# The scores' product with the lower part of q in two 64-row halves of the array, and narrower products of zeros at the start

## The chip, the cores and the metric

The kernel runs on one core of a Trainium2 chip. The metric is the device time of one execution in microseconds (us), the median of several runs. One further execution is recorded by the hardware profiler; every start, duration and wait below comes from that one.

## The reference, cut to what matters

The program is one layer of an encoder: 512 rows of 1024 channels, three branches (a convolution, a differential attention, a spatial gate) that are mixed, and an MLP behind them. The change concerns the attention's scores. For each of 8 heads there are two maps j, each with a head dimension of 64:

```
sc = jnp.einsum("bqhjd,bkhjd->bhjqk", qblk, kf) * scale   # scale = 64 ** -0.5
sc = sc - slopes * dist
p  = jax.nn.softmax(sc, axis=-1)
a  = p[:, :, 0] - lam * p[:, :, 1]
o  = jnp.einsum("bhqk,bkhe->bqhe", a, vf)
```

Queries are taken in 4 blocks of 128, so there are 8 x 4 x 2 = 64 score tiles of 128 x 512.

## The kernel before, in words

All operands of products are float32 numbers split in two: an upper part, rounded to the format that TensorE multiplies in one pass (`float32r`), and a lower part, the rest. A product of two split numbers is three products: upper with upper, upper with lower, lower with upper. Every product goes through `pe.matmul`, a helper at L58, and every transpose through L62, so the profile has these two lines for all of TensorE's work and tells products apart by the names of their tiles. TensorE executes in the order in which the code is written (`keep_in_program_order`); the order on VectorE (DVE) and ScalarE (ACT) is set by a scheduler when the program is built, from priorities and its own estimate of durations. Names that begin with `w_` are weights, `hh`/`hl` the upper and lower part of the normalized input, `ps_a` and `ps_b` PSUM banks, of which there are four of each kind.

**Scores.** `proj_qk(h)` makes q and k of head h. For map j the 64 channels of q lie on partitions 0 to 63 (j = 0) or 64 to 127 (j = 1) of the product's bank. ScalarE writes the upper part `qh` there and VectorE the lower part `ql`; a DMA on SyncE's queue then copies each to the other 64 partitions, so that both halves hold the same. `kk` of map j holds the upper part of k on the same 64 partitions and the lower part of k on the other 64. One product with K = 128 rows of `qh` against `kk` is therefore upper with upper plus upper with lower, and a second one, `ql` against `kk`, adds lower with upper (and lower with lower). `scores(q)` does this for both maps: four products of 512 columns, two to a bank. VectorE then adds the slope term and takes the minimum, ScalarE takes the exponential.

`head(h)` yields between its steps (four times `scores`, four times `turn`, and so on); between the steps the projections of the next heads are issued as fill, so that TensorE has other products while VectorE and ScalarE work on the scores.

**Start.** While the input is loaded and normalized, `keep_warm(n)` issues n products of a tile of zeros, 512 columns wide: 26 ahead of the first transposes of the normalized input, 3 and 2 further on. `norm_x(t)` normalizes 128 rows (t = 0 to 3): a square sum on ScalarE, a short chain that ends in `hs` on VectorE (L303), eight transposes on TensorE (L62), and the copies `hh` (ScalarE, L223) and `hl` (VectorE, L224). Weights are split by ScalarE (`w_hi`, L150) and VectorE (`w_lo`, L151). The first three weight units are multiplied with rows 0 to 255 before the transposes of t = 2 and t = 3 are all done: unit, transposes of t = 2, unit, transposes of t = 3, unit.

Lines that the change and the prediction touch: the two score products (L500 and L501 of the code, L58 in the profile), L457 and L458 (the two copies by DMA), L275 to L284 (the zeros), L303 and L151 at the start. One more place is needed to read the prediction: the transposes of `prow` (128 rows) and of `cw`, the convolution's weights, which have only 32 rows, at L341 to L344.

Of the kernel before, what the change touches and what calls it, by code (L numbers as in the profile page):

```python
# [16 lines left out]
P = 128  # L17
S = 512
# [30 lines left out]
def encoder_layer(ctx: ExitStack, tc: tile.TileContext, a: dict, out: bass.AP):  # L49
    nc = tc.nc  # L50
# [13 lines left out]
    def mk(name, bufs=1, **kw):  # L64
        return tc.tile_pool(name=name, bufs=bufs, reuse_waits="tile", **kw)

    def f32(ap):
        return ap.bitcast(F32)
# [101 lines left out]
    def bank(tag):  # L170
        return ps["pool"].tile([P, 512], F32, tag=tag, bufs=ps[tag], name=f"ps_{tag}")
# [42 lines left out]
    def to_T(src, hi, lo, tt):  # L214
        for half in range(2):
            b = bank("b")
            for j in range(4):
                kt = half * 4 + j
                pe.transpose(b[:, j * P:(j + 1) * P], src[:, kt * P:(kt + 1) * P], ident)
            b3 = b.rearrange("p (k t) -> p k t", t=P)  # L220
            c = slice(half * 4, half * 4 + 4)
            tk = slice(tt * P, (tt + 1) * P)
            ev = act.activation(hi[:, c, tk], b3, AF.Copy)  # L223
            vec.tensor_tensor(lo[:, c, tk], b3, f32(hi[:, c, tk]), op=ALU.subtract)  # L224
        return ev.ins
# [43 lines left out]
    with mk("p0") as p0:  # L269
        gpre = p0.tile([P, D], F32, tag="gpre", name="gpre")  # L270
        act.dma_start(gpre, a["norm_mix_pre"].partition_broadcast(P))
        warm = p0.tile([P, 1], F32, tag="warm", name="warm")
        act.activation(warm, eps_t, AF.Sqrt)
        zero = p0.tile([P, S], F32R, tag="zero", name="zero")
        vec.memset(f32(zero[:, :]), 0.0)  # L275

        def keep_warm(n):

            b = bank("b")
            for _ in range(n):  # L280
                pe.matmul(b, zero[:, 0:P], zero, start=True, stop=True)

        keep_warm(26)
        xt = []  # L284
        for t in range(TT):
            xx = p0.tile([P, D], F32, tag="xx", bufs=4, name="xx")
            nc.sync.dma_start(xx, x[t * P:(t + 1) * P, :])
            xt.append(xx)
            if t == W0AT:
                load_to(1)  # L290

        evac = {}

        def norm_x(t):
            sq = p0.tile([P, D], F32, tag="sq", bufs=2, name="sq")
            ss = p0.tile([P, 1], F32, tag="ss", bufs=4, name="ss")
            i = act.activation(sq, xt[t], AF.Square, accum_out=ss)
            if t > 1:
                tc.add_manual_dep(i.ins, evac[t - 2].name, mybir.DependencyInfo(
                    mybir.DependencyClass.NoSync, mybir.DependencyReason.DATA), reason="order")  # L300
            r = rstd_of(p0, ss, 1.0 / D)
            hs = p0.tile([P, D], F32, tag="hs", bufs=2, name="hs")
            vec.scalar_tensor_tensor(hs, xt[t], r, gpre, op0=ALU.mult, op1=ALU.mult)  # L303
            evac[t] = to_T(hs, hh, hl, t)


        hT = (hh, hl)
        norm_x(0)
        keep_warm(3)
        norm_x(1)  # L310
        keep_warm(2)
        first = take(3, 0)
        fb = [bank("a") for _ in first]
        for n, w in enumerate(first):
            if n == 0:

                for i, (sw, m) in enumerate(((0, 0), (1, 0), (0, 1))):
                    for kt in range(KT):
                        pe.matmul(fb[0][:, 0:256], w[sw][:, kt], hT[m][:, kt, 0:256], start=i + kt == 0,
                                  stop=(i, kt) == (2, KT - 1))  # L320
            else:
                run(unit_gen(fb[n][:, 0:256], w, hT, slice(0, 256)))
            if n < 2:
                norm_x(2 + n)
        for n, w in enumerate(first):
            run(unit_gen(fb[n][:, 256:512], w, hT, slice(256, 512)))


        rowsrc = [("conv_b", 8), ("conv_ln_g", 8), ("conv_ln_b", 8), ("b_gate", 24), ("subln_g", 1), ("sgu_b", 8)]
        prow = p0.tile([P, P], F32, tag="prow", name="prow")  # L330
        pool.memset(prow, 0.0)
        off, col = 0, {}
        for n, k in rowsrc:
            pool.dma_start(prow[off:off + k, :], a[n].rearrange("(r c) -> r c", c=P) if len(a[n].shape) == 1 else a[n])
            col[n] = off
            off += k
        cw = p0.tile([32, D], F32, tag="cw", name="cw")
        pool.memset(cw, 0.0)
        pool.dma_start(cw[0:CK, :], a["conv_w"])
        pcol = cq.tile([P, P], F32, tag="pcol", name="pcol")  # L340
        b = bank("b")  # L341
        pe.transpose(b[:, 0:P], prow, ident)
        for c in range(KT):
            pe.transpose(b[:, P + c * 32:P + (c + 1) * 32], cw[:, c * P:(c + 1) * P], ident[0:32, 0:32])  # L344
        vec.tensor_copy(pcol, b[:, 0:P])
        convw = cq.tile([P, KT, 32], F32, tag="convw", name="convw")
        vec.tensor_copy(convw, b[:, P:P + KT * 32].rearrange("p (k j) -> p k j", j=32))

        def pc(n, i=0):
            return pcol[:, col[n] + i:col[n] + i + 1]  # L350

        sub08 = cq.tile([P, 1], F32, tag="sub08", name="sub08")
        vec.tensor_scalar(sub08, pc("subln_g"), 1.0 - LAM_INIT, None, op0=ALU.mult)
# [56 lines left out]
    b = bank("a")  # L410
# [33 lines left out]
    def proj_qk(h, got):  # L444


        wq, wk = take(2)
        bq = bank("a")
        yield from unit_gen(bq, wq, hT)
        qh = ap_.tile([P, 2, S], F32R, tag="qh", bufs=2, name="qh")  # L450
        ql = ap_.tile([P, 2, S], F32R, tag="ql", bufs=2, name="ql")
        for j, (s0, s1) in enumerate(((0, 64), (64, 0))):
            src = bq[s0:s0 + 64, :]
            hi, lo = qh[s0:s0 + 64, j], ql[s0:s0 + 64, j]
            act.activation(hi, src, AF.Copy, scale=-SCALE)
            vec.scalar_tensor_tensor(lo, src, -SCALE, f32(hi), op0=ALU.mult, op1=ALU.subtract)
            nc.sync.dma_start(f32(qh[s1:s1 + 64, j]), f32(qh[s0:s0 + 64, j]))  # L457
            nc.sync.dma_start(f32(ql[s1:s1 + 64, j]), f32(ql[s0:s0 + 64, j]))  # L458
        bk = bank("a")
        yield from unit_gen(bk, wk, hT)  # L460
        kk = ap_.tile([P, 2, S], F32R, tag="kk", bufs=2, name="kk")
        for j, (s0, s1) in enumerate(((0, 64), (64, 0))):
            src = bk[s0:s0 + 64, :]
            act.activation(kk[s0:s0 + 64, j], src, AF.Copy)
            vec.tensor_tensor(kk[s1:s1 + 64, j], src, f32(kk[s0:s0 + 64, j]), op=ALU.subtract)
        got["qk", h] = qh, ql, kk
# [18 lines left out]
    def head(h, got):  # L485

        qh, ql, kk = got["qk", h]
# [7 lines left out]
        def scores(q):  # L495
            tk = slice(q * P, (q + 1) * P)
            ex = []
            for j in range(2):
                b = bank("b")
                pe.matmul(b, qh[:, j, tk], kk[:, j], start=True, stop=False)  # L500
                pe.matmul(b, ql[:, j, tk], kk[:, j], start=False, stop=True)  # L501
                m = ap_.tile([P, 1], F32, tag="m", bufs=6, name="m")
                vec.tensor_tensor_reduce(b, b, nal[:, 384 - q * P:896 - q * P], 1.0, 3.0e38,  # L503
                                         ALU.add, ALU.min, m)
                e = ap_.tile([P, S], F32, tag="e", bufs=4, name="e")
                l = ap_.tile([P, 1], F32, tag="l", bufs=6, name="l")
                act.activation(e, b, AF.Exp, bias=m, scale=-1.0, accum_out=l)  # L507
                r = ap_.tile([P, 1], F32, tag="r", bufs=6, name="r")
                vec.reciprocal(r, l)
                ex.append((e, r))  # L510
            c1 = ap_.tile([P, 1], F32, tag="c1", bufs=4, name="c1")
            vec.tensor_tensor(c1, ex[1][1], nlam, op=ALU.mult)
            at = ap_.tile([P, S], F32, tag="at", bufs=4, name="at")
            act.activation(at, ex[0][0], AF.Copy, scale=ex[0][1])
            vec.scalar_tensor_tensor(at, ex[1][0], c1, at, op0=ALU.mult, op1=ALU.add)
            ats[q] = at
# [13 lines left out]
        b = bank("b")  # L530
# [6 lines left out]
        b = bank("b")  # L537
# [16 lines left out]
    for h in range(H):  # L554
        n = 0
# [62 lines left out]
    for h in range(H):  # L618
        next(fill)
        next(fill)  # L620
        b = bank("a")
# [96 lines left out]
    for g in range(KT):  # L718
        (w,) = take(1)
        gc = slice(g * P, (g + 1) * P)  # L720
        b = bank("b")
# [429 lines left out]
    for q in range(1, FT // 4):  # L1151
# [20 lines left out]
        s1 = snap(ba)  # L1172
# [88 lines left out]
    s1 = e_ = v6 = w7 = None  # L1261
    for n, step in enumerate(seq[:-TAIL]):
# [8 lines left out]
        if step == ("p1", 3):  # L1271
            s1 = [snap(b) for b in bd]
# [65 lines left out]
```

## Time and profile before

| | |
|---|---|
| median of 3 runs | 1060.08 us (1059.95 to 1060.1) |
| the profiled execution | 1059.99 us, of which span 1058.2 us |
| TensorE products busy | 1042.6 us of the span (99%) |
| TensorE weight loads busy | 900.0 us (85%) |
| VectorE busy | 827.0 us (78%) |
| ScalarE busy | 580.5 us (55%) |
| mean granted TensorE clock | 0.998 |

A busy share says how long an engine had work, not how long others waited for it. PE stands for TensorE's products, PEld for its weight loads, which run beside products. The end of a product is modelled, some 0.16 us late, so the distance from the start of one to the start of the next is what a product costs in a row of them. The profiled execution lies 0.09 us below the median and has 1.8 us outside the span.

### The profile page before, as it was taken

The numbers are of one execution on the slowest core, as the hardware profiler recorded it, in microseconds if no ns is written. First come the engines' busy times: TensorE is split into PE (matmuls) and PEld (weight loads), VectorE is DVE, ScalarE is ACT, GpSimd is POOL, SyncE is SP. The second block draws the span as 40 slices with busy tenths as digits, with TensorE's granted clock in tenths as the row PEclk, the third lists the DMA queues.
The fourth block names the chain that finished last, engine by engine and source line by source line (L and its number), as shares of the span: only waits on it lengthen the run. The fifth ranks groups of instructions, "written<-read, shape, count | busy, mean of one in ns | idle before, by whom it ended". The sixth has DMA issues, their size and how long they took to land.

```text
span 1058.2 us, 14724 instructions
## 1 busy us (share of the span) xinstructions
PE 1042.6 (99%) x5688; PEld 900.0 (85%) x5688; DVE 827.0 (78%) x1296; ACT 580.5 (55%) x902; POOL 24.3 (2%) x41
## 2 busy tenths in 40 slices
PE   8999999999999999999999999999999999999997
PEld 7989898888878888888888888888999999888885
DVE  6696887968997697999899546457988889867746
ACT  5456677766673752344322493344677787555531
POOL 3000000000000000000000000000000001100000
PEclk9999999999999999999999999999999999999999
DMA  7342323223232333322333214463343319724532
GB/s 227 84 139 61 100 81 100 80 81 87 73 120 87 92 112 90 99 81 80 100 100 99 80 45 135 132 226 138 112 150 101 122 43 265 150 80 139 178 121 80
DMA packets 138391, 118.15 MB, mean 112 GB/s; under 512 B 4166, under 2 KB 116850, under 8 KB 138321
## 3 DMA queue, kind: packets, MB, share of 16 engines
q1 hardware_dynamic: 133120, 103.82, 32.1%
q0 software_dynamic: 4480, 11.82, 4.8%
q10 hardware_dynamic: 720, 1.57, 0.4%
q8 instruction: 44, 0.72, 0.3%
q14 instruction: 27, 0.21, 0.1%
HBM read 108.81 MB, written 4.19 MB: 107 GB/s over the span
## 4 chain that ended last, share of the span: by engine, by line
PE 91%; DVE 5%; ACT 2%; issue 1%; DMA 1%; DVEq 0%; ACTq 0%
PE ps_a L58 69%; PE ps_b L58 19%; PE ps_b L62 3%; DVE w_lo L951 1%; DMA xx<-in_x_dram 1%; DVE us L1257 0%; DVE w_lo L151 0%; ACT y L751 0%; DVE hs L303 0%; DVE jk L827 0%; PE ps_a L62 0%; DVE hl L224 0%; ACT jk L825 0%; DVE jk L1247 0%; DVE rs_s L206 0%
## 5 line engine op out<-in xcount | busy, mean ns | idle before, releaser
L150 ACT ACTIVATE w_hi<-w_raw 128x1024 fp32r<-128x1024 f32 x116 | 122.9, 1059 | 214.0 <-PE ps_a L58 177.4
L58 PE MATMUL ps_a<-hh,w_hi 128*128 128x512 f32 (+1 forms) x536 | 205.4, 385 | 0.0
L58 PE MATMUL ps_a<-hh,w_lo 128*128 128x512 f32 (+1 forms) x536 | 202.9, 381 | 0.0
L58 PE MATMUL ps_a<-hl,w_hi 128*128 128x512 f32 (+1 forms) x536 | 202.5, 380 | 0.0
L372 DVE SCALAR_TENSOR_TENSOR acc<-apad,convw,acc 128x512 f32<-128x512 f32 x232 | 173.5, 748 | 5.0
L151 DVE TENSOR_TENSOR w_lo<-w_raw,w_hi 128x1024 fp32r<-128x1024 f32 x116 | 141.5, 1220 | 41.5 <-ACT w_hi L150 41.2
L58 PEld LDWEIGHTS ps_a<-hh,w_lo 128*128 128x128 f32 x536 | 100.3, 188 | 19.6
L58 PEld LDWEIGHTS ps_a<-hl,w_hi 128*128 128x128 f32 x536 | 100.4, 188 | 18.3
L58 PEld LDWEIGHTS ps_a<-hh,w_hi 128*128 128x128 f32 x536 | 100.4, 188 | 18.2
L58 PE MATMUL ps_a<-ring,w_hi 128*128 128x256 f32 x336 | 57.9, 276 | 0.0
L58 PEld LDWEIGHTS ps_a<-ring,w_hi 128*128 128x128 f32 x336 | 50.6, 188 | 0.0
L58 PE MATMUL ps_a<-h2h,w_lo 128*128 128x256 f32 x176 | 48.8, 277 | 1.4 <-DVE w_lo L951 1.4
L58 PE MATMUL ps_a<-w_hi,hh 128*128 128x256 f32 (+1 forms) x160 | 49.7, 311 | 0.0
L58 PE MATMUL ps_a<-h2h,w_hi 128*128 128x256 f32 x176 | 49.0, 278 | 0.0
L58 PE MATMUL ps_a<-h2l,w_hi 128*128 128x256 f32 x176 | 48.8, 277 | 0.0
L58 PE MATMUL ps_a<-w_hi,hl 128*128 128x256 f32 (+1 forms) x160 | 48.7, 304 | 0.0
L58 PE MATMUL ps_a<-w_lo,hh 128*128 128x256 f32 (+1 forms) x160 | 48.6, 304 | 0.0
L507 ACT ACTIVATE e<-ps_b,m 128x512 f32<-128x512 f32 x64 | 43.4, 681 | 7.3 <-DVE m L503 7.0
L58 PE MATMUL ps_a<-ring,w_lo 128*128 128x256 f32 x168 | 46.5, 277 | 0.2 <-DVE w_lo L951 0.2
L58 PE MATMUL ps_a<-w_hi,ring 128*128 128x512 f32 x144 | 45.5, 389 | 0.0
L503 DVE CUSTOM_DVE_ANT_0 ps_b<-ps_b,al 128x512 f32<-128x512 f32 x64 | 43.5, 698 | 0.5 <-PE ps_b L58 0.2
L951 DVE TENSOR_TENSOR w_lo<-w_raw,w_hi 128x1024 fp32r<-128x1024 f32 x28 | 33.7, 1220 | 8.3 <-ACT w_hi L947 8.3
(304 smaller groups left out, 2431.6 us busy)
## 6 DMA issues: line engine op xcount, KB each, us to landing
w_raw<-in_w_in_dram SPq DMA_DIRECT2D x80, 512.0 KB, 3.7
w_raw<-in_w_ffn_up_dram SPq DMA_DIRECT2D x32, 512.0 KB, 4.6
w_raw<-in_w_ffn_down_dram SPq DMA_DIRECT2D x28, 512.0 KB, 4.1
w_raw<-in_w_proj_attn_dram SPq DMA_DIRECT2D x8, 512.0 KB, 4.0
w_raw<-in_w_proj_sgu_dram SPq DMA_DIRECT2D x8, 512.0 KB, 4.1
w_raw<-in_w_proj_conv_dram SPq DMA_DIRECT2D x8, 512.0 KB, 4.1
w_raw<-in_w_out_dram SPq DMA_DIRECT2D x8, 512.0 KB, 3.6
t<-in_w_ffn_down_dram SPq DMA_DIRECT2D x8, 512.0 KB, 5.7
```

Of the source, the lines that this page charges most:

```text
L58: return tc.keep_in_program_order(nc.tensor.matmul(*args, **kw))
L62: return tc.keep_in_program_order(nc.tensor.transpose(*args, **kw))
L150: act.activation(hi, raw, AF.Copy)
L151: vec.tensor_tensor(lo, raw, f32(hi[:, :]), op=ALU.subtract)
L372: vec.scalar_tensor_tensor(o, apad[:, c, j:j + S], convw[:, c, j:j + 1], acc, op0=ALU.mult, op1=ALU.add)
L503: vec.tensor_tensor_reduce(b, b, nal[:, 384 - q * P:896 - q * P], 1.0, 3.0e38, ALU.add, ALU.min, m)
L507: act.activation(e, b, AF.Exp, bias=m, scale=-1.0, accum_out=l)
L951: order(vec.tensor_tensor(lo, raw, f32(hi[:, :]), op=ALU.subtract))
```

## The change

Three things change. The lower part of q is no longer copied to the other 64 partitions. Its product takes only the 64 partitions on which q's channels lie, for map 0 the rows 0 to 63 and for map 1 the rows 64 to 127 of the array, against the upper part of k on the same rows (lower with lower falls away); and the four products of a step are reordered, first both with `qh`, then both with `ql`, with both banks taken ahead of them. At the start 26 products of zeros become 24, and eight of 128 columns follow in a bank of their own.

```
-        def keep_warm(n):
+        def keep_warm(n, m=S):
 
             b = bank("b")
             for _ in range(n):
-                pe.matmul(b, zero[:, 0:P], zero, start=True, stop=True)
-
-        keep_warm(26)
+                pe.matmul(b[:, 0:m], zero[:, 0:P], zero[:, 0:m], start=True, stop=True)
+
+        keep_warm(24)
+        keep_warm(8, P)
...
             nc.sync.dma_start(f32(qh[s1:s1 + 64, j]), f32(qh[s0:s0 + 64, j]))
-            nc.sync.dma_start(f32(ql[s1:s1 + 64, j]), f32(ql[s0:s0 + 64, j]))
...
+            bs = [bank("b") for _ in range(2)]
             for j in range(2):
-                b = bank("b")
-                pe.matmul(b, qh[:, j, tk], kk[:, j], start=True, stop=False)
-                pe.matmul(b, ql[:, j, tk], kk[:, j], start=False, stop=True)
+                pe.matmul(bs[j], qh[:, j, tk], kk[:, j], start=True, stop=False)
+            for j, r_ in enumerate((slice(0, 64), slice(64, 128))):
+                pe.matmul(bs[j], ql[r_, j, tk], kk[r_, j], start=False, stop=True)
+            for j in range(2):
+                b = bs[j]
```

On TensorE, at the first step of the first head, the program of before has the products of the two maps one after the other (a number behind a name tells buffers apart; what a row waits for stands in brackets):

```order
L58 MATMUL ps_b_803<-kk_766,qh_731 128x512 [waits DMAHW1_49,DVE_49]
L58 MATMUL ps_b_803<-kk_766,ql_732 128x512 [waits DMAHW3_49]
L58 MATMUL ps_b_813<-kk_766,qh_731 128x512 [waits DMAHW4_49,DVE_49]
L58 MATMUL ps_b_813<-kk_766,ql_732 128x512 [waits DMAHW5_49]
L58 MATMUL ps_a_783<-hh_88,w_hi_695 128x512
```

At the same place the changed program has both products with the upper part first, and the next unit behind the two with the lower part:

```order
L58 MATMUL ps_b_808<-kk_771,qh_738 128x512 [waits DMAHW1_49,DVE_49]
L58 MATMUL ps_b_809<-kk_771,qh_738 128x512 [waits DMAHW3_49,DVE_49]
L58 MATMUL ps_b_808<-kk_771,ql_739 128x512
L58 MATMUL ps_b_809<-kk_771,ql_739 128x512
L58 MATMUL ps_a_788<-hh_88,w_hi_702 128x512
```

The product with map 1 of `kk` has moved ahead of the product of map 0 with `ql`, and the two with `ql` wait for nothing of their own. The same swap is made at all 32 steps; the order of the other products on TensorE is the same in both programs.

On VectorE the scheduler's order changes in many places. At the start, behind the lower parts of the first 256 rows, the program of before has this, up to the second `w_lo` (`hs` of L303 is the normalized block t = 2):

```order
L151 TENSOR_TENSOR w_lo<-w_raw,w_hi 128x1024
L203 RECIPROCAL rs_r<-rs_s 128x1
L199 TENSOR_SCALAR rs_v<-ss 128x1
L206 SCALAR_TENSOR_TENSOR rs_s<-rs_v,rs_r 128x1
L210 TENSOR_SCALAR rs_s<-rs_s 128x1
L211 TENSOR_TENSOR rs_r<-rs_r,rs_s 128x1
L303 SCALAR_TENSOR_TENSOR hs<-xx,rs_r,gpre 128x1024
L151 TENSOR_TENSOR w_lo<-w_raw,w_hi 128x1024
```

The changed program has this at the same place (one line number further; `hs` of t = 2 and of t = 3 are its two rows of L304):

```order
L151 TENSOR_TENSOR w_lo<-w_raw,w_hi 128x1024 x2
L203 RECIPROCAL rs_r<-rs_s 128x1
L199 TENSOR_SCALAR rs_v<-ss 128x1
L206 SCALAR_TENSOR_TENSOR rs_s<-rs_v,rs_r 128x1
L203 RECIPROCAL rs_r<-rs_s 128x1
L210 TENSOR_SCALAR rs_s<-rs_s 128x1
L206 SCALAR_TENSOR_TENSOR rs_s<-rs_v,rs_r 128x1
L211 TENSOR_TENSOR rs_r<-rs_r,rs_s 128x1
L210 TENSOR_SCALAR rs_s<-rs_s 128x1
L304 SCALAR_TENSOR_TENSOR hs<-xx,rs_r,gpre 128x1024
L211 TENSOR_TENSOR rs_r<-rs_r,rs_s 128x1
L304 SCALAR_TENSOR_TENSOR hs<-xx,rs_r,gpre 128x1024
```

The second `w_lo` and half of the short chain of t = 3 have moved ahead of `hs` of t = 2, and `hs` of t = 3 follows it at once.

## Rows read from the trace of the kernel before

**Rows 1.** The page: its first line, and its parts 1 and 4

```profile
span 1058.2 us, 14724 instructions
PE 1042.6 (99%) x5688; PEld 900.0 (85%) x5688; DVE 827.0 (78%) x1296; ACT 580.5 (55%) x902; POOL 24.3 (2%) x41
...
PE 91%; DVE 5%; ACT 2%; issue 1%; DMA 1%; DVEq 0%; ACTq 0%
```

**Rows 2.** Waits of PE, 60 to 310 us; six windows' sum, 60 to 300 us

```profile
PE ps_b L58 <- DVE kk L465: 0.4, 1, 0.4
...
sum 240.00, PE 239.55 PEld 204.60 DVE 198.29 ACT 166.53 POOL 0.00; mean PE 39.93 PEld 34.10 DVE 33.05 ACT 27.76 POOL 0.00
```

**Rows 3.** Tile ql: count, shortest/median/longest ns, first and last start

```profile
L58 PE MATMUL ps_b<-kk,ql x64: 388/389/398, 68.0 to 293.9; 128*128 128x512 f32 x64
...
L458 SPq DMA_DIRECT2D ql<-ql x16: 461/462/468, 63.0 to 265.6; - x16
```

**Rows 4.** PE's timeline at one step: start, duration, line, names, rows*columns of the array

```profile
75.11 0.39 PE L58 MATMUL ps_b<-kk,qh 128*128 128x512 f32 x1
...
76.02 0.39 PE L58 MATMUL ps_a<-hh,w_hi 128*128 128x512 f32 x1
```

**Rows 5.** The same timeline at the first step of the first head

```profile
68.03 0.39 PE L58 MATMUL ps_b<-kk,ql 128*128 128x512 f32 x1
68.86 0.50 PE L58 MATMUL ps_b<-kk,qh 128*128 128x512 f32 x1 [0.45 <-DVE kk L465]
69.20 0.40 PE L58 MATMUL ps_b<-kk,ql 128*128 128x512 f32 x1
```

**Rows 6.** Timelines of PE, PEld at cw's 32-row transposes; tile cw as in rows 3

```profile
35.60 0.27 PE L62 MATMUL ps_b<-ident,prow 128*128 128x128 f32 x1
35.80 0.68 PE L62 MATMUL ps_b<-ident,cw 32*128 32x32 f32 x8
36.41 0.50 PE L58 MATMUL ps_a<-hh,w_hi 128*128 128x512 f32 x1
36.74 0.40 PE L58 MATMUL ps_a<-hl,w_hi 128*128 128x512 f32 x1
...
35.50 0.14 PEld L62 LDWEIGHTS ps_b<-ident,prow 128*128 128x128 f32 x1
35.80 0.57 PEld L62 LDWEIGHTS ps_b<-ident,cw 32*128 32x128 f32 x8 [0.16 <-issue]
36.41 0.19 PEld L58 LDWEIGHTS ps_a<-hh,w_hi 128*128 128x128 f32 x1
...
L62 PE MATMUL ps_b<-ident,cw x8: 220/222/244, 35.8 to 36.3; 32*128 32x32 f32 x8
```

**Rows 7.** PE's timeline at four 128-row transposes among products of 256 columns

```profile
204.84 0.60 PE L62 MATMUL ps_b<-ident,at 128*128 128x128 f32 x4
205.19 0.36 PE L58 MATMUL ps_a<-w_hi,hh 128*128 128x256 f32 x1
205.39 0.28 PE L58 MATMUL ps_a<-w_lo,hh 128*128 128x256 f32 x1
```

**Rows 8.** The start: timelines of PE, then DVE

```profile
1.46 8.04 PE L58 MATMUL ps_b<-zero 128*128 128x512 f32 x26 [1.46 <-DVE zero L275]
9.84 1.06 PE L62 MATMUL ps_b<-ident,hs 128*128 128x128 f32 x8 [0.35 <-DVE rs_r L203]
18.69 1.06 PE L62 MATMUL ps_b<-ident,hs 128*128 128x128 f32 x8 [1.52 <-DVE hs L303]
23.16 1.09 PE L62 MATMUL ps_b<-ident,hs 128*128 128x128 f32 x8 [0.54 <-DVE hs L303]
...
16.43 0.15 DVE L203 RECIPROCAL rs_r<-rs_s 128x1 f32<-128x1 f32 x1
17.25 1.28 DVE L303 SCALAR_TENSOR_TENSOR hs<-xx,rs_r,gpre 128x1024 f32<-128x1024 f32 x1
18.45 1.22 DVE L151 TENSOR_TENSOR w_lo<-w_raw,w_hi 128x1024 fp32r<-128x1024 f32 x1
```

## The prediction

> **What bounds the kernel now.** I read the page first, then the waits, then the timelines. The page says that TensorE's products are busy for 99% of the span and that 91% of the chain that ended last is PE [rows 1]; a busy share alone would not prove a bound, since product ends are modelled. The waits do: from 60 to 310 us, where all heads lie, PE waited once, for 0.4 us, and VectorE was busy for 198.29 us of the 240 us from 60 to 300 [rows 2]. So in this stage time is what TensorE needs for its list of instructions: an instruction taken out or made dearer there moves the end by its own price. The start is different: there PE waits for the normalized blocks, 0.35, 1.52 and 0.54 us before three of the four groups of transposes [rows 8], and the order on VectorE sets the time.
>
> **What a score product costs.** Four of them and nothing else stand between 75.11 and 76.02 us [rows 4]: 0.91 / 4 = 0.226 us each (0.39 us is the modelled duration). The 64 products with `ql` [rows 3] make 32 pairs of 0.45 us.
>
> **The pair on two halves.** No row shows two products on different rows of the array, so the second half's price is bounded by nothing and by a whole product, 0.226 us. I take nothing: each half has its own rows, weights and bank, and what a product costs elsewhere in the trace is the time to pass its columns through its rows, which two separate halves can do side by side. That saves 0.226 us a pair, 32 x 0.226 = 7.2 us.
>
> **Going into the halves and out again.** The trace has one place where the array changes from 128 rows to fewer and back: the transposes of `cw`, 32 rows each [rows 6]. From the start of `prow` (35.60) to the start of the second product behind them (36.74) it is 1.14 us. Without any cost of the change it would be: one 128-row transpose, 0.11 us ((0.60 - 0.27) / 3 of the four of [rows 7], the 0.27 from [rows 6]); eight of 32 rows at (0.68 - 0.222) / 7 = 0.065, 0.52 us; one product of 512 columns, 0.226. Together 0.86. So 0.28 us go to the change of rows: 0.09 on the way in (0.20 between 35.60 and 35.80 in place of 0.11) and 0.19 on the way out (0.94 - 0.52 - 0.226). The weight loads show why. `prow`'s load began 0.10 us ahead of its product; the first load of `cw` began with its own product, after 0.16 us without a wait that the profile shows, and so did the first load behind `cw` [rows 6]. A change of rows stops the load ahead. That it isn't the change from transposes back to products is seen in [rows 7]: four 128-row transposes and a product of 256 columns take 205.39 - 204.84 = 0.55 us, 4 x 0.11 plus 0.11, nothing more.
>
> What does an uncovered load cost here? After the wait at 68.86 us the next product starts 0.34 us later in place of 0.226 [rows 5]: 0.11 us. The 0.19 on the way out holds it already. On the way in the narrow transposes of `cw` may have hidden it; a product with `ql` has a longer load, so the entry may be 0.09 + 0.11 = 0.20. The round trip thus lies between 0.28 and 0.39 us, and since `cw`'s products are transposes with shorter loads and the way in for `ql` is between the two, I take the middle, 0.335.
>
> A pair: 0.335 - 0.226 = 0.11 us dearer than before, 32 times 3.5 us (bounds 0.054 and 0.164 a pair, 1.7 to 5.2 us). The change has to win 0.226 with one round trip at each of 32 places; that is the step on which the forecast rests.
>
> **The first step.** In the first head `ql` of map 0 ran from 68.03 us while PE had to wait for `kk` of map 1 until 68.86 anyway [rows 5]. In the changed order the product with `kk` of map 1 stands ahead of it, so it comes out of the wait's cover: +0.2 us, once.
>
> **The copies.** Sixteen DMAs of `ql` leave SyncE's queue, 0.46 us of issue each [rows 3]. Weights queued behind them can be loaded earlier, but PE waits for no load in this stage [rows 2]: 0. The later end of bank 0's product delays VectorE's first minimum of a step by about a product; what hides it is the fill between steps, and if that cover failed it would show as PE waiting for `ps_b` or for `at`.
>
> **The start.** Two edits meet here. (a) 26 products of zeros took 8.04 us and ended at 9.50 [rows 8]; two of 0.226 go and eight narrow ones come. Nothing in the trace is a 128-column product of this kind; it costs no less than a 32-column transpose (0.065) and, I assume, no more than a 512-column product (0.226). That ends the zeros 0.07 to 1.36 us later, of which 0.35 us of idle time absorb the first part. I take the 0.11 of a 128-column transpose: 0.42 later, 0.1 us of it visible, which ScalarE's and VectorE's queues swallow: 0. (b) VectorE's new order puts a second `w_lo` ahead of `hs` of t = 2. That `w_lo` took 1.22 us, and three more short operations come with it; five of them took 0.82 us between 16.43 and 17.25 [rows 8], and since the added ones run in the gaps of a dependent chain I count 0.1 each. `hs` of t = 2 starts 1.5 us later than 17.25, and its transposes at about 20.2 in place of 18.69. The unit behind them kept PE until 23.16 - 0.54 = 22.62; now until 24.1. `hs` of t = 3 then follows at once (two times 1.28 from 18.8, done by 21.4) and is ready, so the 0.54 of waiting vanishes: the transposes of t = 3 start at 24.1 in place of 23.16. Cost 1.0 us; 0.6 if the short operations are free, 2.0 if the narrow zeros cost 0.226 each.
>
> **The sum.** 3.5 + 0.2 + 1.0 = 4.7 us on the profiled execution's 1059.99, which is 0.09 below the median: **1064.7 us** (from 1062.5 with 1.7 + 0.2 + 0.6 to 1067.4 with 5.2 + 0.2 + 2.0). A measurement of this kernel can tell about 0.2%, 2.1 us, from no change; the forecast is slower by 0.44%.
>
> **Rivals.** (1) Faster: the change of rows costs a product nothing, because the 512 columns of `qh` ahead leave more time to load than a transpose of 0.11 us did. Then -7.2 + 1.2 = -6.0 and 1054.0 us. It turns on the round trip: below 0.226 - 1.2 / 32 = 0.19 us the kernel gains. Against it: the load at 36.41 also stood behind 0.5 us of transposes and was not begun early [rows 6]. The Trainium skill's page "TensorEngine Tiling (Array Packing)", section Theoretical Speedup, gives a contract dimension of 64 up to twice the speed, which taken alone is this rival; its Key Properties say that a change of tiling mode drains TensorE. The trace agrees with the second by the 0.20 and 0.33 us between starts in [rows 6], and shows nothing of the first.
>
> (2) Half: only one side is paid, about 0.19 us a trip. Then the pairs give -1.2, the start and first step +1.2: 1060.0 us, no change that can be measured.
>
> (3) Slower still: the halves load their weights one after the other, 0.11 us a pair more, 3.5 us: 1068.2; or they don't run together at all, 7.2 us more: 1071.9. For it speaks only that every product in the trace starts a whole product behind the one ahead. Against these the same skill stands with its page "TensorE: Matmul & The Clock Gate" (Part 3, Measured speedup vs the span model): some 4 ns for each further tile in a pack; no row here shows it, and by it 0.1 us would be added to my sum.
>
> VectorE as a new bound is none: even with 7.2 us less it would be busy for 198.29 of 232.8 us [rows 2].
>
> **Chances.** Forecast 0.37, loads one after the other 0.09, no running together 0.07: slower 0.53. Half 0.14: same. Free change of rows 0.33: faster. The range from 1053.5 to 1068.5 holds all but the last slower case and the tails of the others; the likeliest case's own range is 1062.5 to 1067.4.
>
> **What the changed profile would show.** The forecast is right if the two `ql` products (64 rows) start within a few ns of each other, if the load of the first starts with it and not ahead, and if from the first `qh` of a step to the product behind the pair it takes about 1.0 us in place of 0.91. Rival 1 shows some 0.68 us there, with loads begun during `qh`; no running together shows 1.2 or more. At the start the transposes of t = 2 should begin near 20.2 and those of t = 3 near 24.1, without a wait before the latter. I am wrong if PE's waits in 60 to 310 us grow beyond 1 us, since then the new order on VectorE and ScalarE, not the products, would set the time.

## The result, and the profile after

The changed kernel, called after from here on, takes 1069.99 us (median of four runs, 1067.5 to 1072.65); the kernel before, beside it on the same chip, 1060.01 us (four runs, 1059.88 to 1060.1). The ratio is 1.0082 (95% interval 1.006 to 1.0104): slower by 0.8%, 9.98 us, where 4.7 had been forecast. The time lies above the range. The four runs are 1067.5, 1068.75, 1071.24 and 1072.65 us, and this scatter turned out to be a part of the answer. The profiled execution is the last of them.

The page of the changed kernel, its first line and parts 1 and 4 (they answer to [rows 1]):

```profile
span 1070.9 us, 14675 instructions
...
PE 1055.0 (99%) x5694; PEld 898.1 (84%) x5694; DVE 825.9 (77%) x1296; ACT 582.5 (54%) x902; POOL 24.3 (2%) x41
...
PE 92%; DVE 4%; ACT 2%; DMA 1%; issue 1%; SPq 0%; DVEq 0%; ACTq 0%
```

PE still has the whole chain. Its products are busy for 12.4 us more, although 32 pairs now run side by side. The waits of PE from 60 to 310 us ([rows 2]):

```profile
PE ps_b L58 <- DVE kk L465: 0.7, 1, 0.7
```

One wait, as before, 0.2 us longer (0.68 in place of 0.45, both in the first step). So the new order on VectorE and ScalarE makes PE wait no more in the heads, and what was lost there lies inside PE's own list. The tile `ql` of the changed kernel (columns as in [rows 3]), and the idle time ahead of its instructions:

```profile
L58 PEld LDWEIGHTS ps_b<-kk,ql x64: 182/183/183, 71.4 to 302.1; 64*128 64x128 f32 x64
L58 PE MATMUL ps_b<-kk,ql x64: 491/498/502, 71.4 to 302.1; 64*128 64x512 f32 x64
...
  issue: 11.4, 32
```

All 64 products are 64 rows high, and ahead of each of the 32 pairs the weight loads stood still for 11.4 / 32 = 0.36 us without a wait that the profile can name. One step shows it (timelines of PE and then of PEld; they answer to [rows 4]):

```profile
77.77 0.61 PE L58 MATMUL ps_b<-kk,qh 128*128 128x512 f32 x2
78.31 0.50 PE L58 MATMUL ps_b<-kk,ql 64*128 64x512 f32 x2
78.74 0.50 PE L58 MATMUL ps_a<-hh,w_hi 128*128 128x512 f32 x1
79.08 0.39 PE L58 MATMUL ps_a<-hl,w_hi 128*128 128x512 f32 x1
...
77.54 0.41 PEld L58 LDWEIGHTS ps_b<-kk,qh 128*128 128x128 f32 x2
78.31 0.19 PEld L58 LDWEIGHTS ps_b<-kk,ql 64*128 64x128 f32 x2 [0.35 <-issue]
78.74 0.19 PEld L58 LDWEIGHTS ps_a<-hh,w_hi 128*128 128x128 f32 x1 [0.24 <-issue]
```

Read it as a sum. Two products, a pair and one more product stand between 77.77 and 79.08: 1.31 us. Without any cost of the change of rows it would be 4 x 0.226 = 0.90, so the round trip takes 0.41 us, to the rounding of the rows: 0.09 on the way in (78.31 - 77.77 in place of 0.45), 0.20 in the pair (78.74 - 78.31 = 0.43 in place of 0.226), 0.11 behind it (79.08 - 78.74 = 0.34). The two products with `ql` are one row of 0.50 us, no longer than one of them is: the halves do run side by side. Both their loads and the load behind them begin with their own product and not ahead of it.

The first step of the first head, whose counterpart is [rows 5]:

```profile
69.86 0.39 PE L58 MATMUL ps_b<-kk,qh 128*128 128x512 f32 x1
70.93 0.50 PE L58 MATMUL ps_b<-kk,qh 128*128 128x512 f32 x1 [0.68 <-DVE kk L465]
71.36 0.51 PE L58 MATMUL ps_b<-kk,ql 64*128 64x512 f32 x2
```

The start, on PE and then on VectorE ([rows 8]):

```profile
1.46 9.27 PE L58 MATMUL ps_b<-zero 128*128 128x512 f32 x32 [1.46 <-DVE zero L275]
10.56 1.06 PE L62 MATMUL ps_b<-ident,hs 128*128 128x128 f32 x8
19.97 1.20 PE L62 MATMUL ps_b<-ident,hs 128*128 128x128 f32 x8 [2.94 <-DVE hs L304]
20.82 0.56 PE L58 MATMUL ps_a<-hh,w_hi 128*128 128x256 f32 x1
21.18 0.41 PE L58 MATMUL ps_a<-hl,w_hi 128*128 128x256 f32 x1
21.39 0.41 PE L58 MATMUL ps_a<-hh,w_lo 128*128 128x256 f32 x1
...
24.45 0.28 PE L58 MATMUL ps_a<-hh,w_lo 128*128 128x256 f32 x1
24.56 0.28 PE L58 MATMUL ps_a<-hh,w_hi 128*128 128x256 f32 x1
...
18.63 1.28 DVE L304 SCALAR_TENSOR_TENSOR hs<-xx,rs_r,gpre 128x1024 f32<-128x1024 f32 x1
20.02 1.28 DVE L304 SCALAR_TENSOR_TENSOR hs<-xx,rs_r,gpre 128x1024 f32<-128x1024 f32 x1
```

The wait ahead of the transposes of t = 2 has grown from 1.52 to 2.94 us, as the order on VectorE had it. Then comes something new: products of 256 columns start 0.21 us apart (21.18, 21.39), until about 24.2 us, and 0.11 apart from then on (24.45, 24.56). Windows of the changed kernel say why (the last three columns are the granted clock, the DMA share and GB/s):

```profile
0.00:25.00 25.00, 20.40 (x107) 17.92 (x108) 15.38 (x34) 13.20 (x23) 8.91 (x24) 0.93 0.77 240
780.00:900.00 120.00, 118.60 (x1011) 118.40 (x1010) 98.92 (x96) 86.45 (x119) 1.22 (x1) 1.00 0.38 119
```

The granted clock is 0.93 in the first 25 us: at 20.8 us, behind the wait and the eight transposes, it fell to 0.5, which is 1.2 of 2.4 GHz, and it was back at 24.2. In the profile of before it stayed at 1.00 there. The first product with `qh` starts at 69.86 in place of 67.80, 2.06 us late.

The second surprise lies 400 us behind the last score. In the MLP the products of 256 columns with `h2h` last from 727.1 to 881.8 us in before, 154.7 us, and from 735.8 to 894.2 in after, 158.4. Tile `h2h`, its first group in each kernel, after and then before:

```profile
L58 PE MATMUL ps_a<-h2h,w_hi x176: 276/281/387, 735.8 to 894.2; 128*128 128x256 f32 x176
```

```profile
L58 PE MATMUL ps_a<-h2h,w_hi x176: 276/276/388, 727.1 to 881.8; 128*128 128x256 f32 x176
```

The median product has become 5 ns longer, at a granted clock of 1.00 from 780 to 900 us. The order on PE is the same there. The timelines at the same place, after and then before:

```profile
793.78 0.28 PE L58 MATMUL ps_a<-h2h,w_lo 128*128 128x256 f32 x1
...
795.55 0.28 PE L58 MATMUL ps_a<-h2h,w_lo 128*128 128x256 f32 x1
```

```profile
785.25 0.28 PE L58 MATMUL ps_a<-h2h,w_hi 128*128 128x256 f32 x1
...
786.84 0.28 PE L58 MATMUL ps_a<-h2h,w_lo 128*128 128x256 f32 x1
```

Fifteen products further is 1.77 us in after, 0.118 each; fourteen further is 1.59 in before, 0.114 each. So the 12.7 us by which the two profiled executions differ are 2.1 up to the first score, 6.6 up to the end of the attention (its last part, `ob`, starts at 344.8 in place of 336.1, 8.7 late), nothing up to 735.8 (8.7 late), 3.7 in the MLP and 0.3 behind it.

### The profile page after: what moved, and what is told of

Read it like the earlier page. It is cut to its first block, busy times and chain, and to the rows that moved or that the text cites. A ratio compares the mean times of both kernels' runs of the same rounds, so it can differ in the third digit from the quotient of the medians.

```text
span 1070.9 us, 14675 instructions
## 1 busy us (share of the span) xinstructions
PE 1055.0 (99%) x5694; PEld 898.1 (84%) x5694; DVE 825.9 (77%) x1296; ACT 582.5 (54%) x902; POOL 24.3 (2%) x41
## 4 chain that ended last, share of the span: by engine, by line
PE 92%; DVE 4%; ACT 2%; DMA 1%; issue 1%; SPq 0%; DVEq 0%; ACTq 0%
PE ps_a L58 70%; PE ps_b L58 19%; PE ps_b L62 3%; DMA w_raw<-in_w_in_dram 1%; DVE w_lo L954 1%; DVE us L1260 0%; ACT y L754 0%; DVE jk L830 0%; DVE w_lo L151 0%; PE ps_a L62 0%; ACT jk L828 0%; ACT w_hi L150 0%; SPq L288 0%; DVE jk L1250 0%; DVE wk L825 0%
## 5 line engine op out<-in xcount | busy, mean ns | idle before, releaser
L58 PE MATMUL ps_a<-hh,w_hi 128*128 128x512 f32 (+1 forms) x536 | 209.8, 394 | 0.0
```

What stands on the lines that cost most here:

```text
L58: return tc.keep_in_program_order(nc.tensor.matmul(*args, **kw))
```

## The experiments

**Theory A**: the pair saves its 0.226 us, the round trip costs 0.41, and 32 times the difference, 5.9 us, together with the first step is what the heads lose; the start and the MLP's pace are separate matters. **Rivals**: the loss comes from the start or from a new order on VectorE and ScalarE; or the two halves don't run together and the trip is cheap; or the four products' new order costs by itself.

**Only the scores.** The zeros stay at 26 full products; the pair and the missing DMAs are taken over.

```
-        keep_warm(24)
-        keep_warm(8, P)
+        keep_warm(26)
```

> Only the scores' part of the change; the 26 products of zeros of before. Theory A (the halves run together and one trip into the 64-row halves and back costs 0.40 us, as the changed kernel's trace reads): 32 x (0.40 - 0.226) = 5.6 us, about 6.5 with the first step, so 1066.5 us where products of 256 columns keep their pace, and up to 3.8 us more in an execution in which those of the MLP run at 0.118 instead of 0.113 us. Theory B (the loss comes from the new order at the start and its low clock, the scores are nearly free): 1060 to 1062 us. VectorE's order at the start is that of before, so no low clock between 20 and 24 us.

Measured: 1066.6 us (five runs at 1066.5 to 1066.7, one at 1070.61); ratio 1.006 (1.0043 to 1.0078) to 1060.16. The order at the start is that of before, the first `qh` starts at 67.8 as there, and the first `ob` at 342.7: 6.6 us are lost between. Theory A's time came out; its split did not quite. It had some 0.9 us for the first step. The trace has 0.40 there and 31 times 0.18 = 5.6 in the other steps, both up to the second product behind the pair; the remaining 0.5 lies in the products behind that one, which stand up to 0.236 us apart in place of 0.227. The scores' part accounts for 6.5 us.

**Only the zeros.** The scores are those of before.

```
-        keep_warm(26)
+        keep_warm(24)
+        keep_warm(8, P)
```

> Only the products of zeros are changed (24 and eight narrow ones), the scores as before. Theory A: 0.9 us slower, 2.1 in executions in which the clock falls behind the 2.9 us wait for the third block, so 1060.9 to 1062.1 us, and again up to 3.8 more if the MLP's products fall into the slower pace. Theory B: nearly the whole change, 1067 us or more.

Measured: 1062.38 us (twelve runs, 1060.8 to 1067.55); ratio 1.002 (1.0005 to 1.0034). The two quickest runs are 0.6 and 1.0 us above before, as the start alone would have it. Five lie at 1062.2 to 1062.4, and the profiled execution, one of these, has the half clock: 3.41 us of it from 20.0 us on. Of the other five, 1066.15 fits the half clock with the MLP's slower pace on top. The rest (1063.5, 1063.61, 1064.01 and 1067.55) lie above what theory A allows, and what held them up is not shown; the first three have mean clocks of 0.995 and 0.996, where the profiled execution has 0.997. Theory B, 1067 us or more from the zeros alone, has fallen. The zeros' edit alone changes the order on VectorE; with the scores' edit alone it is as before.

**Both products with `ql` on the same half.** Rows 0 to 63 for both maps, with the zeros and the copies of `ql` of before; the second map's small term then takes k's lower part, a change of what is computed.

```
-            for j, r_ in enumerate((slice(0, 64), slice(64, 128))):
+            for j, r_ in enumerate((slice(0, 64), slice(0, 64))):
```

> Like the run with the scores' part alone, but map 1's product with the lower part of q takes rows 0 to 63 as well (with the copies of it kept), so that both products of a step stand on the same half; map 1's operand is then the lower part of k, so the value of that small term changes. Theory A (halves run together): a whole product more a step, 32 x 0.226 = 7.2 us over the run with the scores' part alone, about 1073.7 us. Rival C (the products of the two halves run one after the other anyway, the trip being cheaper than 0.40): the same time as that run, 1066.5 us.

Measured: 1077.94 us (1073.81 to 1078.23, five runs); ratio 1.0143 (1.012 to 1.0166). The two lowest runs (1073.81 and 1074.16) are 7.2 and 7.6 us above the kernel with only the scores, 0.23 us a pair; the other three, the profiled one among them, have the MLP's slower pace or lie where it would put them. Its step:

```profile
79.57 0.61 PE L58 MATMUL ps_b<-kk,qh 128*128 128x512 f32 x2
80.12 0.73 PE L58 MATMUL ps_b<-kk,ql 64*128 64x512 f32 x2
80.77 0.50 PE L58 MATMUL ps_a<-hh,w_hi 128*128 128x512 f32 x1
81.11 0.40 PE L58 MATMUL ps_a<-hl,w_hi 128*128 128x512 f32 x1
```

From 79.57 to 81.11 it is 1.54 us in place of 1.31: on one half the products follow one another, on two they run together. The rival without running together has fallen.

**Two trips a step.** The 64-row products in before's order, `qh`, `ql`, `qh`, `ql`, with the zeros of before.

```
             for j, r_ in enumerate((slice(0, 64), slice(64, 128))):
-                pe.matmul(bs[j], ql[r_, j, tk], kk[r_, j], start=False, stop=True)
+                b = bank("b")
+                pe.matmul(b, qh[:, j, tk], kk[:, j], start=True, stop=False)
+                pe.matmul(b, ql[r_, j, tk], kk[r_, j], start=False, stop=True)
```

> The scores' part alone, in the old order: qh and ql of map 0, then of map 1, each ql on its 64 rows, so the array goes into the halves and back twice a step and no two halves are used side by side. Theory A: 4 x 0.226 + 2 x 0.40 = 1.70 us a step in place of 0.90, 32 x 0.80 = 25.7 us over before, about 1086 us. Rival C (no running together, a trip of about 0.18): 32 x 2 x 0.18 = 11.5 us, about 1071.5 us.

Measured: 1086.49 us (1086.28 to 1086.66); ratio 1.0241 (1.0223 to 1.0259). That is 26.3 us above before for 64 trips and no pair: 0.41 us a trip. The step shows each crossing:

```profile
80.27 0.40 PE L58 MATMUL ps_b<-kk,qh 128*128 128x512 f32 x1
80.60 0.50 PE L58 MATMUL ps_b<-kk,ql 64*128 64x512 f32 x1
81.03 0.50 PE L58 MATMUL ps_b<-kk,qh 128*128 128x512 f32 x1
81.45 0.50 PE L58 MATMUL ps_b<-kk,ql 64*128 64x512 f32 x1
81.88 0.50 PE L58 MATMUL ps_a<-hh,w_hi 128*128 128x512 f32 x1
```

A product between two changes of rows, whichever way they go, is 0.42 to 0.43 us ahead of the next start: 0.20 more than the 0.226 of a product. A crossing costs 0.20 and a round trip two of them.

**Only the order.** `qh`, `qh`, `ql`, `ql` with all 128 rows and all copies.

```
-            for j, r_ in enumerate((slice(0, 64), slice(64, 128))):
-                pe.matmul(bs[j], ql[r_, j, tk], kk[r_, j], start=False, stop=True)
+            for j in range(2):
+                pe.matmul(bs[j], ql[:, j, tk], kk[:, j], start=False, stop=True)
```

> Before, with the four products of a step reordered (both with the upper part of q first, then both with the lower part, all with 128 rows, copies kept). Theory A: the order costs nothing but the first step, 0.2 to 0.5 us, so 1060.2 to 1060.6 us. Theory D (it is the later first bank and the scheduler's new order in the heads, not the rows, that cost the 6.5 us of the scores' part): several us slower, up to 1066 us.

Measured: twelve runs in two groups, six at 1060.33 to 1061.08 and six at 1064.53 to 1064.72; median 1062.81, ratio 1.0015 (1.0 to 1.0029). The lower group's median, 1060.74, is 0.45 above that of before's lower group (1060.29), and in its trace the first step is longer by 0.24 us and the others are as before: the order is nearly free. The two groups are the matter of the MLP's pace, and before has them too: of its 57 runs beside these experiments 16 lie at 1063.9 to 1064.4.

**Two steps share one trip.** Four `qh` into four banks, then four `ql`, all at the place of the first of the two steps; the zeros are those of before.

```
+            bs = {(q, j): bank("b") for q in (q0, q0 + 1) for j in range(2)}
+            for q, j in bs:
+                pe.matmul(bs[q, j], qh[:, j, tks[q]], kk[:, j], start=True, stop=False)
+            for q, j in bs:
+                r_ = slice(j * 64, j * 64 + 64)
+                pe.matmul(bs[q, j], ql[r_, j, tks[q]], kk[r_, j], start=False, stop=True)
```

> The scores' part, with two steps of a head taken together: four products with the upper part of q into four banks, then the four with its lower part on the two halves, so one trip into the halves and back serves four of them; the 26 products of zeros of before. Theory A (the trip is paid per change of rows, 0.40 us): 16 x 0.40 - 32 x 0.226 = -0.8 us, with the first step's 0.5 about 1059.8 us, if VectorE and ScalarE follow with all four banks of a kind filled at once; each wait of TensorE for a bank would come on top. If the price hung on each pair and not on the change of rows: 1066.5 us as with the scores' part alone.

Measured: 1067.71 us (four runs at 1067.6 to 1067.7, two at 1071.8 and 1071.9); ratio 1.0071 (1.005 to 1.0091). A miss by 7.9 us. Two of the sixteen groups, PE's timeline; then PE's waits from 60 to 310 us:

```profile
75.59 1.07 PE L58 MATMUL ps_b<-kk,qh 128*128 128x512 f32 x4
76.58 0.73 PE L58 MATMUL ps_b<-kk,ql 64*128 64x512 f32 x4
77.25 0.50 PE L58 MATMUL ps_a<-hh,w_hi 128*128 128x512 f32 x1
77.58 0.39 PE L58 MATMUL ps_a<-hl,w_hi 128*128 128x512 f32 x1
...
130.69 0.95 PE L58 MATMUL ps_b<-kk,qh 128*128 128x512 f32 x3
132.15 0.50 PE L58 MATMUL ps_b<-kk,qh 128*128 128x512 f32 x1 [0.52 <-DVE ob L547]
132.58 0.73 PE L58 MATMUL ps_b<-kk,ql 64*128 64x512 f32 x4
```

```profile
PE ps_b L58 <- DVE ob L547: 2.0, 4, 0.5
PE ps_b L58 <- DVE kk L464: 0.7, 1, 0.7
PE ps_b L58 <- ACT e L513: 0.7, 4, 0.2
```

The undisturbed group is as theory A has it: 1.99 us from 75.59 to 77.58, of which 7 x 0.226 = 1.58 are products and pairs and 0.41 is one trip for two steps. But a group needs all four `ps_b` banks at once, and in eleven of the sixteen the third or fourth `qh` starts late. Eight of them have a wait in the rows above: the bank is still held by VectorE's copy `ob` or ScalarE's `e`. Summed over the trace, the distances between neighbouring `qh` exceed 0.227 by 8.0 us, 0.8 of it at the first step, where the kernel with only the scores waits for `kk` as well. Behind the late banks the entry into the halves loses its covered load as well: 0.43 to the next start in place of 0.32, 1.2 us over eleven groups. Without the first step that is 7.2 + 1.2 = 8.4 us, where the kernel with only the scores has 0.7; the difference, 7.7, is the miss to 0.2 us. Even undisturbed the gain on before would be small: two steps and the product behind take 9 x 0.227 = 2.04 us there.

**The zeros, with PE kept busy.** Twelve products of zeros ahead of the transposes of t = 2.

```
+            if n == 0:
+                keep_warm(12)
             if n < 2:
                 norm_x(2 + n)
```

> The run with the products of zeros alone, with 12 more products of zeros (512 columns, 2.7 us) in the 2.9 us for which TensorE waits ahead of the third block's transposes. Theory A: the clock no longer falls behind that wait, so the executions around 1062.3 us go to 1060.9 us, with single ones 3.8 us above in the slower pace of the MLP's products. If the clock's fall had another cause than the wait, or cost nothing, the times would stay at 1062.3 us.

Measured: 1060.9 us (nine runs at 1060.65 to 1061.52, three near 1065); ratio 1.0008 (0.9995 to 1.0021). The half clock is gone from the profile, and the common time goes from 1062.3 to 1060.9, 1.4 us less, although twelve products more run.

**The whole change with the same twelve products.**

> The whole change with twelve products of zeros added ahead of the transposes of t = 2, the place where PE waited 2.94 us for hs. Theory (clock at the start, and two paces in the MLP): the stretch at granted clock 0.5 is gone; the quick executions lie at the scores-only kernel's 1066.5 plus the 0.9 that the same fill left of the zeros' edit, 1067.4 us, none lie 1.3 above that, and about a third lie 3.8 above it, at 1071.2. Rival (the half clock isn't what set after's four times apart): executions at 1068.7 and 1072.6 remain.

Measured: 1067.23 to 1067.42 in four runs, 1071.27 and 1071.3 in two, nothing between; median 1067.4, ratio 1.0063 (1.0039 to 1.0086). The start of its profile:

```profile
17.20 2.90 PE L58 MATMUL ps_b<-zero 128*128 128x512 f32 x12
20.17 1.06 PE L62 MATMUL ps_b<-ident,hs 128*128 128x128 f32 x8
...
23.94 1.03 PE L62 MATMUL ps_b<-ident,hs 128*128 128x128 f32 x8
...
68.52 0.39 PE L58 MATMUL ps_b<-kk,qh 128*128 128x512 f32 x1
```

No run lies where the clock's fall would put it, at 1068.7 or 1072.6. With that, after's four runs can be read, though only the last of them has a profile: 1067.5 with neither effect, 1068.75 with the clock's fall, 1071.24 with the slower pace in the MLP, 1072.65 with both. The recorded mean clocks agree: 0.997 in the two with the fall, 0.999 and 0.998 in the others.

**The MLP's waits covered.** In the first group of the MLP PE waits for `w_lo` at two places; 5 and 13 spare products, written to a bank that nobody reads, stand ahead of them, in the kernel above and in before.

```
+        n_ = {2: 5, 4: 13}.get(i, 0) if q == 1 else 0
+        if n_:
+            spare = bank("b")
+        for _ in range(n_):
+            pe.matmul(spare[:, 0:256], w[0][:, 0, 0:P], m[0][:, 0], start=True, stop=True)
```

> The kernel with the twelve zeros, and in addition 5 and 13 spare products of 256 columns (the upper weights, into a bank that nobody reads) ahead of the two products of the MLP's first group at which PE waited for w_lo, 0.65 and 1.68 us from start to start. Theory P (the slower pace of the 256-column products is entered where PE starts again after these waits): with PE kept busy there no execution is slow, all lie at 1067.4 us within 0.6. Rival (the pace is set by something else): a third of the executions still lie 3.8 us above the rest, near 1071.2.

> The kernel before with the same 5 and 13 spare products in the MLP and nothing else. Theory P: all executions at 1060.0 us within 0.6, while about a fifth of the kernel before itself lie near 1064. Rival: a fifth to a third of this kernel's too lie near 1064.

Measured, on the kernel above: two runs at 1069.0 and four from 1073.16 to 1075.02 (median 1073.9, ratio 1.0097, 1.0072 to 1.0123). On before: seven runs at 1061.5 to 1061.7 and five from 1065.6 to 1066.3 (median 1061.66, ratio 1.0013, 0.9996 to 1.0029). Both groups stay, so theory P's forecast did not come true. The three highest of the first four lie 5.6 to 6.0 us above the two lowest, at mean clocks of 0.996 and 0.997; that is more than the pace takes elsewhere, and why is not shown. The profile of the first kernel, one of its two quick runs, shows that only the first wait went away (waits of PE, 760 to 800 us):

```profile
PE ps_a L58 <- DVE w_lo L956: 1.9, 1, 1.9
```

The second stayed, since VectorE's `w_lo` for it itself starts 1.55 us later than without the spare products (791.92 in place of 790.37). So the slow pace comes without the first wait too, as far as the profiled execution stands for the others; whether it needs the second was not reached, and what sets the pace stays open. The traces do say where it begins. In the three profiles in which it lasts to the end of `h2h`, it begins where PE starts again behind one of these waits: behind the second in after (793.0 us) and with both `ql` on the same half (798.1), behind the first with two steps on one trip (776.8). With the zeros alone a slow stretch begins behind the first (771.2) and ends behind the second (786.6). So theory P is not refuted: the wait that was left standing is one at which the pace was seen to change.

## Why the prediction was wrong, step by step

Two things failed. The round trip was mis-sized, 0.41 us a trip where 0.335 was taken. And two effects stood in no term of the sum, the fall of the clock behind the longer wait and the MLP's slower pace; these two carried the median past the upper end of the range.

**What bounds it**: right. PE's own list set the time of the heads; its waits there grew by 0.2 us.

**The pair on two halves**: right. The products start together, and putting them on one half costs 0.23 us a pair more.

**The round trip**: this step failed, by its size. It was bounded by 0.28 and 0.39 us and taken at 0.335, "since `cw`'s products are transposes with shorter loads"; it measures 0.41, by 64 trips as well as by the starts of one step, just beyond the upper bound. The upper bound's argument was nearly right: 0.09 on the way in, 0.11 for a load that nothing covers, 0.19 on the way out. What went wrong is the step from `cw` to `ql`: with `cw` little of an uncovered load shows on the way in (its first two transposes start 0.085 us apart, the others 0.062), and half of it was therefore left out. Here the full 0.11 shows, behind a product of 512 columns. That the narrow transposes hide it is likely, but not shown, since no trace has them without a change of rows. The pair's loss is therefore 0.41 - 0.226 = 0.18 and not 0.11: 5.8 us in place of 3.5, and 0.5 more in the products behind, which the sum did not have. It decides the sign of the whole change: the pair wins 7.2 us and 32 trips cost 13.

The rule that fits is the one of the Trainium skill's page "TensorEngine Tiling (Array Packing)", Key Properties, that a change of mode drains TensorE. These traces show 0.20 us a crossing, and not what the time goes into. The same skill's page "TensorE: Matmul & The Clock Gate" (Part 3, The mechanism) says that a load overlaps with products in flight only where its rows differ from theirs. Here the two loads of a pair, on different rows, do begin together (78.31), but loads on the same 128 rows overlap as well (77.54, two loads begun before the second `qh`), and at each change of rows none begins ahead (78.31 and 78.74).

**The first step**: 0.2 forecast. From its first `qh` to the product behind the pair it now takes 71.80 - 69.86 = 1.94 us; `ql` no longer runs under the wait for `kk` [rows 5]. Measured to the second product behind, a step became 0.18 longer on the mean of the other 31 and this one 0.40, so 0.2 is right once the pair's own 0.18 is taken off; the new order alone, with 128 rows, made it 0.24 longer.

**The copies**: nothing, as forecast; PE waits for no load and no `ps_b`.

**The start**: the order on VectorE did what was read from it. In the whole change with the twelve products, without the fall of the clock, the transposes of t = 2 and t = 3 start at 20.17 and 23.94 (forecast 20.2 and 24.1) and the first score 0.72 us late (forecast 1.0). The narrow zeros cost 0.11 each, as assumed. The zeros end at 10.73 us in the profile of after (1.46 + 9.27), 0.8 later than the forecast had it, since there the full ones stand 0.43 apart until 7.2 us, and in before and in the whole change with the twelve products until 5.4. The following wait swallows it. What the step did not see is that the longer wait lets the clock fall: 1.3 us, in two of the four runs. The wait's length could have been worked out from [rows 8]: 20.2 less the end of the unit ahead, 18.69 - 1.52 = 17.17, is 3.0 us, and 2.94 were measured. Its consequence could not, since before shows no fall in this stage.

**The MLP's pace**: not in the prediction. It adds 3.7 to 4.0 us to two of the four runs of after and to 16 of 57 runs of before, none of which was among the runs shown ahead. So the change did not bring it; whether it makes it more frequent can't be told from four runs. With the clock's fall it lifted this median above the range.

The sum by what was measured: 6.5 for the scores and 0.8 for the start, 7.3 us, so 1067.4, where 4.7 was forecast; the clock and the pace bring the median of four to 1070.0. The size of the loss that belongs to the change, 7.3 us, lies at the upper end of the likeliest case's range; that this range held it is in part luck, since the pair with the products behind lost 6.3 where at most 5.2 was allowed, and the start lost less than its upper bound. Of the rivals "loads one after the other" came nearest in time (1068.2), but not in its mechanism: the loads of a pair are one row of 0.19 us.

No version tried here beats the kernel before. With the scores alone it takes 1066.6 us; where two steps share a trip, 1067.7, since PE then waits for banks.

## What to carry to other kernels

A product on part of the rows is not free where it stands alone among full ones: price the way in and the way out first, and pack only where one trip is shared by enough products that their saving (here 0.226 us a pair) exceeds it (0.41 us). Before sharing a trip, count the PSUM banks that it holds at once and who frees them. When an edit at the start lengthens a wait on PE, look at the granted clock behind it; cheap products in the gap can be worth more than they cost.

## What the runs showed of the hardware that was not expected

- A change between 128 and 64 rows costs 0.20 us in either direction (64 trips: 26.3 us), and at each change the first weight load begins with its product and not ahead. Of the 0.20, 0.11 is what the missing load costs, as far as it costs what it did behind a wait (0.34 in place of 0.226 in [rows 5]). Two products on different halves start 1 to 5 ns apart in these traces, most of them 3 to 4.
- After a wait of 2.8 or 2.9 us on PE the granted clock went to half for 3.4 us in the two profiles that have this wait, and by the times in part of the executions only; with twelve products of zeros in the gap it did not, in the two profiles that have them.
- The same stream of 256-column products runs at 0.113 or at 0.118 us apart at a granted clock of 1.00, and the slower one can last for 100 us (793 to 894 us in after's profile). Which it takes differs from run to run of the same program. In the three profiles in which it lasts it begins behind a wait of PE; its cause is open.
